# Loads in written order, a later start of the side loads, up factors kept on chip and a ring of three gate tiles in a hybrid HGRN2 and short-convolution block

## The chip, the core and the metric

One core of a Trainium2 chip runs the whole kernel in one launch. TensorE (PE in the profile) multiplies, VectorE (DVE) and ScalarE (ACT) work on tiles in SBUF, GpSimd (POOL) and SyncE (SP) mostly issue transfers. The metric is the device time of one launch in microseconds; the time before is the median of three runs.

## What is computed

The input x is 1024 positions by 2048 channels, all float32. Cut to what matters:

```
mod = silu(c) @ w_ada + b_ada ;  shift, scale, gate = split(mod, 3)
h = rms_norm(x, g_pre) * (1 + scale) + shift
q, f, i, z_a, bb, cc, vb, z_b = split(h @ w_in, 8)            # 8 x 1024 columns
y_a = rms_norm(hgrn2_chunkwise(q, log f, 1 - f, i), g_head_a) * silu(z_a)
y_b = bb * causal_depthwise_conv(cc * vb) * silu(z_b)
m_a, m_b = split(sigmoid(h @ w_merge + b_merge), 2)           # 2 x 2048 columns
out = (m_a * (y_a @ w_up_a) + m_b * (y_b @ w_up_b)) @ w_o
return x + gate * rms_norm(out, g_post)
```

## The kernel before

Every large product is done in float32 as three matmuls of reduced-precision parts: each operand is split into a high part (a cast on ScalarE) and a low part (a subtraction on VectorE), and high x high, high x low and low x high are added in PSUM (`mm3`, `split_w`, `split_h`). The blocks are multiplied by a seven-product scheme (the products are called p1, p6, p2, p7, p5, p4, p3), so sums and differences of blocks, the factors, are formed on VectorE first.

The stages, in order:

- Opening. 16 pieces of x are loaded, normalised and transposed into xT. `ada_pair(q)`, for q = 0 to 3, loads 16 pieces of w_ada (512 KB each, tile `ada_raw`), multiplies them with silu(c) on TensorE (into `prow`) and VectorE (into `row_v`), and turns the two rows into columns of scale and shift (`pa`, `a_c`, `sh_c`). `factors_a` then scales xT and forms the factors of four products for two of eight groups at a time.
- First sweep. 48 units (`unit_a`), one per pair of 128 columns of w_in and w_merge. Each loads four weight tiles (`w_raw`, five buffers), and does products p1, p6, p2 and p7, 96 matmuls of 128x512. Sums go to DRAM (`s_scr`, `u_scr`) for the second sweep. Beside the units run `factors_b` (the factors of p5, p4, p3, stored to `hb_scr`), `gate_step` (w_ada's third part, 32 loads called `ga_raw`) and `sums_o` (sums of w_o, 32 loads called `wo`).
- Second sweep. The same 48 units with p5, p4 and p3, 72 matmuls each, and the recurrent heads and the convolution. From unit 33 on `y_factors` loads y of a branch, forms its seven factors for four groups (tile `yp`) and stores them to `yf_scr`.
- Up b and up a (`up`): the products with w_up_b, then w_up_a. Each first loads its 28 factors (7 products x 4 groups, 512 KB each) from `yf_scr`, then runs eight steps `du` of seven products, 84 matmuls. In a step the products are combined in `o2` and `ut` and multiplied by two gate tiles `g`, loaded on POOL's queue from `g_scr`. Up b stores the results to `pb_scr`; up a adds them back (`merge`, tile `pb`) and stores to `m_scr`.
- Last stage: the product with w_o, the last norm, the store.

Two things set the order. Transfers wait in order in the queue that issues them: most loads in SP's, stores and gate loads in POOL's. Instructions of each engine are put in order by a scheduler that runs the program through a timeline of its own; only what is marked with `keep_in_program_order` stays as written, and `issue_after` holds what is inside it behind a given instruction. At most eight loads are under way from SP's queue: the ninth is issued when the first has landed. Most large tiles (x, xT, w_ada pieces, factors, y, gates) share one pool of 38 buffers of 128x1024 (`big`), so a load also waits until such a buffer is released.

## Time and profile before

| | |
|---|---|
| median of three runs | 2771.5 us (2767.51 to 2771.66) |
| the profiled run | 2769.2 us |
| its span | 2767.5 us |
| mean granted TensorE clock | 0.984 |
| TensorE busy | 97% of the span |
| VectorE busy | 62% |
| ScalarE busy | 33% |
| read from and written to HBM | 431.04 MB, 198.18 MB |

The profile was taken in the run of 2769.2 us. TensorE's busy share is near the whole span, so the mean shares say little; the table of windows, which counts each engine's instructions in a stretch, shows where TensorE is behind its own pace. A window's row begins with the stretch and its length in us, then gives busy us and the number of instructions in brackets for PE, PEld, DVE, ACT and POOL, then the granted clock (1.00 is 2.4 GHz, 0.50 is 1.2 GHz), the busy share of the transfer engines and GB/s. A busy share a little above 1 means that they are full.

### The profile page before, as it was taken

What the parts mean: (1) busy time and instruction counts of PE and PEld (TensorE: products, weight loads), DVE (VectorE), ACT (ScalarE), POOL (GpSimd) and SP (SyncE); (2) the same over time, 40 slices, a digit from 0 to 9 for tenths busy, and PEclk for the clock granted to TensorE, in tenths of its full rate; (3) what the DMA queues carried; (4) which work ended last, traced back from release to release, by engine and by line L of the source; (5) the groups of instructions that cost most, each with busy time, mean ns of one, the idle gap of its engine ahead of it and who ended that gap; (6) DMA issues with size and microseconds to landing.
All of it is one profiled execution on the core that took longest, in us unless ns stands there. A gap on an engine that the chain in (4) does not pass through costs nothing.

```text
span 2767.5 us, 31307 instructions
## 1 busy us (share of the span) xinstructions
PE 2673.0 (97%) x11851; PEld 2152.7 (78%) x11851; DVE 1716.7 (62%) x2096; ACT 906.3 (33%) x1176; POOL 280.0 (10%) x495
## 2 busy tenths in 40 slices
PE   4889999999999999999999999999998999999997
PEld 3267878888888888888888888888885787888786
DVE  6777886754554444546666666656563666765667
ACT  4433222222222222233344444435442222232333
POOL 2012111110000000010000000002111101100000
PEclk9899999999999999999999999999998999999999
DMA  9769999985556655584444444359999569773353
GB/s 361 286 201 313 345 349 364 346 292 179 179 192 179 182 175 177 174 316 137 133 130 133 138 146 138 110 178 374 360 363 407 187 213 335 235 282 99 99 178 142
DMA packets 420071, 631.30 MB, mean 228 GB/s; under 512 B 19564, under 2 KB 281808, under 8 KB 419792
## 3 DMA queue, kind: packets, MB, share of 16 engines
q1 hardware_dynamic: 358528, 394.31, 44.7%
q0 software_dynamic: 60208, 230.78, 21.7%
q10 hardware_dynamic: 1184, 4.20, 0.4%
q8 instruction: 93, 1.52, 0.2%
q14 instruction: 58, 0.48, 0.0%
HBM read 431.04 MB, written 198.18 MB: 227 GB/s over the span
## 4 chain that ended last, share of the span: by engine, by line
PE 81%; issue 8%; DMA 7%; DVE 2%; POOL 1%; ACT 1%; DVEq 0%; POOLq 0%; ACTq 0%; SPq 0%
PE po L866 10%; PE pz L119 7%; PE pz L122 7%; PE pz L123 7%; PE px L119 6%; PE px L123 6%; PE px L122 6%; PE py L123 6%; PE py L119 6%; PE py L122 6%; PE pw L119 4%; PE pw L122 4%; PE pw L123 4%; DMA yp<-yf_scr 3%; DMA ga_raw<-in_w_ada_dram 2%
## 5 line engine op out<-in xcount | busy, mean ns | idle before, releaser
L130 ACT CAST w_hi<-w_raw 128x1024 fp32r<-128x1024 f32 (+1 forms) x296 | 290.9, 983 | 1001.6 <-PE px L122 402.5
L131 DVE TENSOR_TENSOR w_lo<-w_raw,w_hi 128x1024 fp32r<-128x1024 f32 (+1 forms) x296 | 335.7, 1134 | 273.1 <-ACT w_hi L130 263.4
L123 PE MATMUL py<-fp,w_lo 128*128 128x512 f32 x768 | 301.2, 392 | 6.9 <-DVE w_lo L131 6.9
L123 PE MATMUL px<-fp,w_lo 128*128 128x512 f32 x768 | 300.9, 392 | 5.2 <-DVE w_lo L131 5.2
L119 PE MATMUL px<-fp,w_hi 128*128 128x512 f32 x768 | 301.2, 392 | 0.0
L122 PE MATMUL py<-fp,w_hi 128*128 128x512 f32 x768 | 299.5, 390 | 1.3 <-DVE fp L136 1.3
L119 PE MATMUL py<-fp,w_hi 128*128 128x512 f32 x768 | 299.8, 390 | 0.9 <-ACT w_hi L130 0.9
L122 PE MATMUL px<-fp,w_hi 128*128 128x512 f32 x768 | 300.0, 391 | 0.0
L866 PE MATMUL po<-w_hi,lt 128*128 128x512 f32 x896 | 244.2, 390 | 0.6 <-DVE og L900 0.6
L866 PEld LDWEIGHTS po<-w_hi,lt 128*128 128x128 f32 x896 | 168.1, 188 | 37.2 <-DVE og L900 2.2
L130 ACT CAST w_hi<-s 128x512 fp32r<-128x512 f32 (+1 forms) x112 | 90.1, 805 | 285.9 <-PE py L122 245.5
L123 PEld LDWEIGHTS py<-fp,w_lo 128*128 128x128 f32 x768 | 144.5, 188 | 41.5 <-DVE w_lo L131 11.2
L123 PEld LDWEIGHTS px<-fp,w_lo 128*128 128x128 f32 x768 | 144.8, 188 | 36.9 <-DVE w_lo L131 6.5
L122 PEld LDWEIGHTS py<-fp,w_hi 128*128 128x128 f32 x768 | 144.5, 188 | 32.1 <-DVE fp L136 1.7
L122 PEld LDWEIGHTS px<-fp,w_hi 128*128 128x128 f32 x768 | 145.1, 189 | 30.8 <-issue 0.5
L119 PEld LDWEIGHTS px<-fp,w_hi 128*128 128x128 f32 x768 | 144.9, 189 | 30.8 <-issue 0.7
L119 PEld LDWEIGHTS py<-fp,w_hi 128*128 128x128 f32 x768 | 144.5, 188 | 30.8 <-ACT w_hi L130 1.3
L119 PE MATMUL pz<-fp,hi 128*128 128x512 f32 x384 | 152.5, 397 | 3.0 <-DVE d L701 3.0
L122 PE MATMUL pw<-fp,w_hi 128*128 128x512 f32 x384 | 150.8, 393 | 0.0
L119 PE MATMUL pz<-fp,w_hi 128*128 128x512 f32 x384 | 150.5, 392 | 0.0
L123 PE MATMUL pz<-fp,lo 128*128 128x512 f32 x384 | 150.4, 392 | 0.0
L119 PE MATMUL pw<-fp,w_hi 128*128 128x512 f32 x384 | 150.4, 392 | 0.0
(286 smaller groups left out, 4959.4 us busy)
## 6 DMA issues: line engine op xcount, KB each, us to landing
w_raw<-in_w_in_dram SPq DMA_DIRECT2D x160, 512.0 KB, 5.2
s_scr<-s POOLq DMA_DIRECT2D x96, 512.0 KB, 6.0
s_raw<-s_scr SPq DMA_DIRECT2D x96, 512.0 KB, 4.3
w_raw<-in_w_merge_dram SPq DMA_DIRECT2D x80, 512.0 KB, 5.7
u_scr<-o POOLq DMA_DIRECT2D x48, 768.0 KB, 7.5
ada_raw<-in_w_ada_dram SPq DMA_DIRECT2D x64, 512.0 KB, 10.8
yf_scr<-yp POOLq DMA_DIRECT2D x56, 512.0 KB, 9.0
yp<-yf_scr SPq DMA_DIRECT2D x56, 512.0 KB, 12.8
```

The source lines that it names most:

```text
L119: mm = nc.tensor.matmul(o, ah, bh, start=first, stop=False, skip_group_check=True)
L122: nc.tensor.matmul(o, ah, bl, start=False, stop=False, skip_group_check=True)
L123: nc.tensor.matmul(o, al, bh, start=False, stop=last, skip_group_check=True)
L130: nc.scalar.copy(out=hi, in_=raw)
L131: nc.vector.tensor_sub(out=lo, in0=raw, in1=hi.bitcast(F32))
L866: nc.tensor.matmul(o, a, b[:, c], start=st, stop=sp, skip_group_check=True)
```

## The change

- Opening. A helper `load` pins a load in written order on SP. The loads of x, of w_ada, of the weights of units 0 and 1, of the gates' w_ada part and of w_o go through it. w_ada pieces of q = 0, 1, 2 use the shared pool only; of q = 3 every fourth has a tile of its own. The row tiles move into a weight buffer.
- Unit 0 is split: three of its weight splits and the loads of its weights stand ahead of `ada_pair(3)`, and its products p1, p6 and p2 run on factors 0 to 5 first, then on 6 and 7, once the last factors are issued.
- First sweep. `factors_b` runs with units 2 to 16, held behind the unit's last sum; `gate_step` with units 10 to 25; `sums_o` with units 26 to 40 (before: units 0 to 15, 16 to 31, 32 to 46, as far as the scheduler left them there).
- Sides of the second sweep. Branch a's factors for all groups come first, branch b's second; p1 of branch b stays on chip (`first_y`, four tiles), so up b loads 24 factors.
- Up. Gate tiles come from a ring of three buffers of their own instead of the shared pool. `merge`'s loads of pb are pinned.

```diff
+    def load(o, i):
+        tc.keep_in_program_order(nc.sync.dma_start(out=o, in_=i))
...
-        if n_ada[0] % 3:
+        if q < 3 or n_ada[0] % 4:
             raw = bigt(F32, "ada_raw").rearrange("p (k e) -> p k e", k=2)
         else:
-            raw = ph.tile([P, 2, HS], F32, tag="ada", name="ada_raw", bufs=4)
-        nc.sync.dma_start(out=raw, in_=w_ada_v[:, k:k + 2, t, q * HS:(q + 1) * HS])
+            raw = ph.tile([P, 2, HS], F32, tag="ada", name="ada_raw", bufs=2)
+        load(raw, w_ada_v[:, k:k + 2, t, q * HS:(q + 1) * HS])
...
+    def unit_a(u, raws):
...
+        if u == 0:
+            v.tensor_sub(out=a21, in0=a11, in1=a21)
+            w2 = split_w(a12, out_t=(ph.tile([P, 8, P], F32R, name="hi3a", bufs=1), wp.tile([P, 8, P], F32R, tag="raw", name="lo3a", bufs=5)))
+            yield
+            p2 = ps("mm", "p2")
+            for gs in (range(6), (6, 7)):
+                for p, w, f in ((px, w1, "p1"), (py, w6, "p6"), (p2, w2, "p2")):
+                    product(p, w, fa[f], pin=True, gs=gs)
...
     for q in range(1, 4):
+        if q == 3:
+            first = unit_a(0, load_a(0))
+            next(first)
         ada_pair(q)
         factors_a((2 * q - 2, 2 * q - 1))
-    factors_a((6, 7), vec=(7,))
+    with tc.issue_after(factors_a((6, 7), vec=(7,)).ins):
+        next(first, None)
...
     for u in range(NU):
-        unit_a(u)
-        if u < 16:
-            if u % 2 == 0:
-                factors_b(u // 2)
-        elif u < 32:
-            gate_step(2 * u - 32)
-            gate_step(2 * u - 31)
-        elif u % 2 == 0:
-            sums_o((u - 32) // 2)
+        if u:
+            for _ in unit_a(u, load_a(u)):
+                pass
+        if u in range(2, 18, 2):
+            with tc.issue_after(last_sum[0]):
+                factors_b(u // 2 - 1)
+        if 10 <= u < 26:
+            gate_step(2 * u - 20)
+            gate_step(2 * u - 19)
+        elif u in range(26, 42, 2):
+            sums_o((u - 26) // 2)
...
                 split_h(t, factor(s, ys[0], ys[1], lambda: small("t2")), nc.scalar.copy)
+                if br and s == "p1":
+                    first_y.append(t)
+                    continue
...
-    side = [f for g in range(4) for br in (1, 0) for f in y_factors(br, g)]
+    first_y = []
+    side = [f for br in (0, 1) for g in range(4) for f in y_factors(br, g)]
...
-        fy = {s: [pair(f"y{s}_{g}") for g in range(4)] for s in STAGES}
+        fy = {s: [pair(f"y{s}_{g}") for g in range(4)] for s in STAGES if not (y0 and s == "p1")}
+        if y0:
+            fy["p1"] = first_y
...
-                t = bigt(F32, "g")
+                t = ph.tile([P, S], F32, tag="g", name="g", bufs=3)
...
-            nc.sync.dma_start(out=t, in_=pb_scr[2 * du + j])
+            tc.keep_in_program_order(nc.sync.dma_start(out=t, in_=pb_scr[2 * du + j]))
```

SP's queue in the opening, behind the last piece of x. A piece of w_ada is named by a running number: before, 714 and 716 are the first two in written order, 722, 732, 746 and 756 later ones of q = 0, and 1175 to 1329 weights of units 0 and 1.

```order
L180 DMA x_7_1_429<-in_x_dram 128x1024
L224 DMA ada_raw_722<-in_w_ada_dram 128x2x512
L224 DMA ada_raw_732<-in_w_ada_dram 128x2x512
L224 DMA ada_raw_746<-in_w_ada_dram 128x2x512
L224 DMA ada_raw_756<-in_w_ada_dram 128x2x512
L325 DMA w_raw_1175<-in_w_in_dram 128x8x128
L325 DMA w_raw_1177<-in_w_in_dram 128x8x128
L325 DMA w_raw_1179<-in_w_in_dram 128x8x128
L325 DMA w_raw_1181<-in_w_in_dram 128x8x128
L325 DMA w_raw_1329<-in_w_in_dram 128x8x128
L224 DMA ada_raw_714<-in_w_ada_dram 128x2x512
```

The same place in the changed kernel, where 712 is the first piece.

```order
L119 DMA x_7_1_428<-in_x_dram 128x1024
L119 DMA ada_raw_712<-in_w_ada_dram 128x2x512
L119 DMA ada_raw_714<-in_w_ada_dram 128x2x512
L119 DMA ada_raw_720<-in_w_ada_dram 128x2x512
L119 DMA ada_raw_722<-in_w_ada_dram 128x2x512
```

The pieces now follow in written order, and the weights of unit 0 have moved back, to where the pieces of q = 2 end (961 and 963) and those of q = 3 begin (1047):

```order
L119 DMA ada_raw_961<-in_w_ada_dram 128x2x512
L119 DMA ada_raw_963<-in_w_ada_dram 128x2x512
L119 DMA w_raw_1017<-in_w_in_dram 128x8x128
L119 DMA w_raw_1019<-in_w_in_dram 128x8x128
L119 DMA w_raw_1021<-in_w_in_dram 128x8x128
L119 DMA w_raw_1023<-in_w_in_dram 128x8x128
L119 DMA ada_raw_1047<-in_w_ada_dram 128x2x512
```

The first gate loads stand in SP's queue before between the weights of unit 6 (26 weight tiles have been issued):

```order
L365 DMA ga_raw_3640<-in_w_ada_dram 128x2x512
L325 DMA w_raw_2052<-in_w_in_dram 128x8x128
L365 DMA ga_raw_3645<-in_w_ada_dram 128x2x512
L365 DMA ga_raw_3786<-in_w_ada_dram 128x2x512
L365 DMA ga_raw_3790<-in_w_ada_dram 128x2x512
L365 DMA ga_raw_3931<-in_w_ada_dram 128x2x512
L325 DMA w_raw_2054<-in_w_in_dram 128x8x128
```

and now between those of unit 13 (53 have been issued):

```order
L311 DMA w_raw_3077<-in_w_in_dram 128x8x128
L119 DMA ga_raw_2761<-in_w_ada_dram 128x2x512
L311 DMA w_raw_3079<-in_w_in_dram 128x8x128
L119 DMA ga_raw_2766<-in_w_ada_dram 128x2x512
L119 DMA ga_raw_2907<-in_w_ada_dram 128x2x512
L311 DMA w_raw_3081<-in_w_in_dram 128x8x128
```

They have moved by seven units, and the 32nd of them stands behind unit 25's weights where it stood behind unit 11's.

POOL's queue at the start of up b. Gates g_scr16 and g_scr17 are those of step 0, 18 and 19 of step 1, 20 and 21 of step 2; pb_scr0 and pb_scr1 are the results of step 0, and so on. Before:

```order
L740 DMA g_14662<-g_scr18_223 128x1024
L740 DMA g_14664<-g_scr19_224 128x1024
L740 DMA g_14801<-g_scr20_225 128x1024
L664 DMA g_scr30_235<-d1_14309 128x1024
L740 DMA g_14803<-g_scr21_226 128x1024
L740 DMA g_14940<-g_scr22_227 128x1024
L740 DMA g_14942<-g_scr23_228 128x1024
L740 DMA g_15079<-g_scr24_229 128x1024
L781 DMA pb_scr1_238<-g_14525 128x1024
L781 DMA pb_scr0_237<-g_14523 128x1024
```

and after:

```order
L773 DMA g_14644<-g_scr18_223 128x1024
L693 DMA g_scr30_235<-d1_14299 128x1024
L814 DMA pb_scr1_238<-g_14507 128x1024
L814 DMA pb_scr0_237<-g_14505 128x1024
L814 DMA pb_scr2_239<-g_14644 128x1024
L773 DMA g_14646<-g_scr19_224 128x1024
L773 DMA g_14783<-g_scr20_225 128x1024
L773 DMA g_14785<-g_scr21_226 128x1024
L814 DMA pb_scr3_240<-g_14646 128x1024
L773 DMA g_14922<-g_scr22_227 128x1024
L814 DMA pb_scr5_242<-g_14785 128x1024
L773 DMA g_14924<-g_scr23_228 128x1024
```

Nine gates were asked for ahead of the first result's store; now three are, and the second gate of step 1 (g_scr19) stands behind the store of that step's first result (pb_scr2).

## Rows read from the trace of the kernel before

**Rows 1.** The page, busy us of TensorE, its share of the span, instructions.

```profile
PE 2673.0 (97%) x11851; PEld 2152.7 (78%) x11851; DVE 1716.7 (62%) x2096; ACT 906.3 (33%) x1176; POOL 280.0 (10%) x495
```

**Rows 2.** Windows: pace of TensorE in five stretches.

```profile
142.00:174.00 32.00, 25.86 (x97) 20.00 (x97) 26.80 (x36) 12.56 (x18) 2.73 (x5) 0.89 0.52 159
174.00:450.00 276.00, 268.07 (x1161) 218.40 (x1160) 219.71 (x254) 74.99 (x95) 43.46 (x81) 0.99 0.97 329
500.00:550.00 50.00, 50.00 (x222) 41.42 (x221) 32.31 (x30) 12.17 (x15) 6.94 (x13) 1.00 1.04 349
2050.00:2200.00 150.00, 136.40 (x544) 105.76 (x543) 72.66 (x107) 40.05 (x57) 20.92 (x39) 0.91 0.88 331
2250.00:2350.00 100.00, 95.46 (x406) 75.67 (x405) 64.59 (x95) 22.61 (x39) 9.15 (x17) 0.98 0.84 310
```

**Rows 3.** Waits of TensorE: us in total, times, longest us.

```profile
PE prow L235 <- DMA ada_raw<-in_w_ada_dram: 19.5, 4, 15.6
...
PE py L123 <- DVE w_lo L131: 7.5, 6, 2.7
PE pz L119 <- DMA yp<-yf_scr: 6.5, 6, 2.5
```

**Rows 4.** Timeline of SP's queue, opening: start us, us, what, how many.

```profile
16.14 4.21 SPq L224 DMA_DIRECT2D ada_raw<-in_w_ada_dram  x4
24.48 10.04 SPq L325 DMA_DIRECT2D w_raw<-in_w_in_dram  x5
34.56 91.41 SPq L224 DMA_DIRECT2D ada_raw<-in_w_ada_dram  x60
```

**Rows 5.** Windows: the opening.

```profile
0.00:142.00 142.00, 96.73 (x323) 39.28 (x323) 98.18 (x177) 61.08 (x97) 16.56 (x21) 0.87 0.89 315
...
56.00:72.00 16.00, 0.50 (x2) 0.00 (x0) 1.62 (x3) 0.00 (x0) 0.00 (x0) 0.65 1.05 387
...
92.00:132.00 40.00, 36.48 (x100) 9.84 (x99) 32.44 (x56) 20.33 (x31) 0.00 (x0) 0.91 0.99 361
```

**Rows 6.** Timeline of TensorE, end of the opening.

```profile
138.62 0.87 PE L235 MATMUL prow<-ada_raw,c_act 128*1 128x512 f32 x1
...
142.04 0.48 PE L119 MATMUL px<-fp,w_hi 128*128 128x512 f32 x1
```

**Rows 7.** Transfers issued from 0 to 150 us: KB each, median us to landing.

```profile
ada_raw<-in_w_ada_dram SPq DMA_DIRECT2D x64, 512.0 KB, 10.8
```

**Rows 8.** Groups by line, 100 to 145 us: busy us, mean ns of one.

```profile
L136 DVE TENSOR_TENSOR fp<-xT,fp 128x512 fp32r<-128x512 f32 x16 | 10.2, 682 | 0.0
```

**Rows 9.** VectorE's waits from 174 to 450 us, and SP's queue there.

```profile
DVE s L338 <- DMA w_raw<-in_w_in_dram: 19.1, 8, 5.3
...
265.57 7.98 SPq L365 DMA_DIRECT2D ga_raw<-in_w_ada_dram  x4
```

**Rows 10.** Timelines of SP and POOL at up b's start, and a window.

```profile
2099.17 5.44 SPq L728 DMA_DIRECT2D yp<-yf_scr  x5
...
2110.62 12.23 SPq L728 DMA_DIRECT2D yp<-yf_scr  x6
...
2107.20 0.55 POOL L740 DMA_DIRECT2D g<-g_scr  x1 [2.98 <-PE pz L123]
...
2117.04 0.54 POOL L740 DMA_DIRECT2D g<-g_scr  x1 [1.76 <-DMA g<-g_scr]
...
2108.00:2140.00 32.00, 23.77 (x71) 14.85 (x70) 10.75 (x17) 4.50 (x7) 4.83 (x9) 0.72 1.03 409
```

**Rows 11.** Transfers issued from 2020 to 2180 us.

```profile
yf_scr<-yp POOLq DMA_DIRECT2D x15, 512.0 KB, 9.0
```

**Rows 12.** The gate tile, 2100 to 2320 us (ns min/median/max), its landing; the copy.

```profile
L771 DVE TENSOR_TENSOR g<-g,o x9: 1217/1220/1226, 2146.7 to 2316.4; 128x1024 f32<-128x1024 f32 x9
L776 DVE TENSOR_TENSOR g<-g,ut x9: 679/684/687, 2155.7 to 2318.2; 128x512 f32<-128x512 f32 x9
...
DMA to landing us min/median/max: 2.9/6.4/20.1
...
L758 ACT COPY o<-px 128x512 f32<-128x512 f32 x6 | 3.5, 587 | 12.5 <-PE px L123 9.0 <-DVE g L771 3.5
```

98 lines of the change are left out of this document (52 added, 46 removed).

## The prediction, made before the changed kernel ran

> **What bounds the kernel now.** I read the page's busy shares first: TensorE is busy 97% of the span [rows 1], so nothing is won except where it stands still or runs slowly. Where that is comes from the table of windows, by counting matmuls. A window in the middle of the first sweep holds 222 in 50 us at a full granted clock [rows 2], 0.225 us each. Against that pace: 142 to 174 us holds 97 where 142 fit, 45 x 0.225 = 10.1 us lost; 174 to 450 us holds 1161 where 1225 fit, 14.5 us; 2050 to 2200 us (end of sweep two, start of up b) 544 of 666, 27.5 us; 2250 to 2350 us (from up b into up a) 406 of 444, 8.6 us. With the opening, whose first product starts at 142.04 us [rows 6], that is where time can be had; the rest of the span runs at pace. The waits of TensorE [rows 3] name what it stood for: w_ada pieces (19.5 us, 15.6 of it at once), a split's low part on VectorE, and y factors coming back from DRAM.
>
> In the opening the queue of SP shows why: four w_ada loads, then ten microseconds in which five weight tiles of units 0 and 1 are issued one by one, then sixty w_ada loads up to 125.97 us [rows 4]. From 56 to 72 us TensorE starts 2 matmuls while the transfer engines are full at 387 GB/s [rows 5]: what it needs is somewhere behind. Then from 73 to 142 us they have stretches with little to do: all in all 315 GB/s over the first 142 us [rows 5].
>
> **Opening, about -19 us.** All loads now stand in the order of use, and the queue is 16 x + 48 w_ada + 4 weight tiles + 16 w_ada = 84 loads of 524,288 bytes. At 387 GB/s one takes 1.355 us, so 113.8 in all; with the first issue at 0.8 and some 3 us for the first to land, the last lands at 117.6. Before, the last was issued at 125.97 and landed a median 10.8 us later [rows 7], 136.8; the last prow matmul began at 138.62 and the first product at 142.04, 5.2 behind the landing [rows 6]. The same tail puts it at 122.8: -19.2. Loads 23 to 44 wait for the slots of x tiles that the transposes release, by my reading up to 5 us behind the pace; the seven loads in flight cover 7 x 1.355 = 9.5 us, so I charge nothing; without that cover it is those 5 us. Bounds: the slowest rate of a full stretch, 361 GB/s at 92 to 132 us [rows 5], makes 84 x 1.452 = 122.0 and leaves -11; a shorter tail gives -22. The DMA page of the Trainium skill (DMA: Bandwidth & Descriptors, section "Bandwidth") says that between HBM and SBUF some 358 GB/s binds. The row of 387 GB/s speaks against it for one core alone; by 358 GB/s the sum would have -10 here in place of -19.
>
> **Unit 0, -7.5 us.** It now starts with three products on factors 0 to 5, 54 matmuls or 12.2 us, where it had two, 36 or 8.1 us, and their splits stand ahead of the last ada_pair. In that time factors 6 and 7 must come: 6 activations and 8 splits, each a cast on ScalarE and a subtraction on VectorE; 8 x 0.68 [rows 8] is 5.4 us there. So most of the 10.1 us goes; I leave 2.5 for the first matmuls at 1.2 GHz (granted clock 0.89 in that window). Bounds -3 to -10.
>
> **Units 1 to 12, -10 us of 14.5.** Loads of ga_raw stand in SP's queue from 265 us on, between the weights of units 6 to 11 [rows 9], and with their 512 KB each the engines are full; VectorE waits 19.1 us for w_raw there [rows 9]. Now they come with units 10 to 26, two per unit, and one unit's own traffic (4 weights, s, u: 3.9 MB in 21.7 us, 181 GB/s) plus two gate loads is 229 GB/s; with the w_o sums, later, 277, well under 387. Those sums get longer time, not more work. What hides the moved loads is the slack of later units; if it is gone, waits like those of before come back there. But TensorE's stops in this stretch end with VectorE's w_lo [rows 3], some of them at units 2 and 3, before any ga_raw load. I put those down to factors_b on VectorE, which is now held behind the unit's last sum, and count on half of them. Bounds -5 to -13.
>
> **Up b, -16 us of 27.5.** Its 28 factor loads ran 1.28 us apart ((5.44 - 0.32) / 4) while alone, and 2.4 us apart ((12.23 - 0.32) / 5) from 2110 us, when POOL had put nine gate loads beside them from 2107 us on [rows 10]. The engines are full, share 1.03 at 409 GB/s from 2108 to 2140 us [rows 10], and TensorE got 71 matmuls there, half of it at 1.2 GHz (clock 0.72). Now p1 of four groups stays on chip: 4 loads and 4 stores less; and the gates have a ring of three, so six of nine gate loads leave this stretch. Ten transfers of 524,288 bytes at 409 GB/s are 12.8 us that the last factor comes earlier, and with the waits the slow matmuls go: 16. Against it: the queue of branch a's first ten factor loads now follows at once, but behind, in the same queue; and branch b's factors are made last, so its stores end just ahead of their loads (15 such stores of both branches from 2020 us on, 9.0 us to landing [rows 11]). The first of these loads is p6, needed 2.7 us later than p1 was. Bounds -5 to -24.
>
> **Up a, -5 us of 8.6**: ten rather than seven of its factor loads come ahead, and four or more gate loads no longer share the engines. Bounds 0 to -8.6.
>
> **The ring of three, +12 us.** In up b, gates of step 0 and the first of step 1 fill it. The second gate of step 1 stands on POOL's queue behind the store of step 1's first result, which is written after the last product of step 1. Then: 0.69 + 0.68 for the two sums on VectorE, twice 0.54 for the issues, 6.4 to landing (2.9 to 20.1), 1.22 for the product of gate and o2, and 0.59 for the next copy into o2, which has one buffer [rows 12]; 10.7 us after the end of step 1. Step 2's third product adds to the PSUM that this copy must have read; it is due after two products, 24 x 0.225 = 5.4 us. TensorE stops some 5 us. Queued behind the waiting product on VectorE is all of step 2's combining; behind the load on POOL both gates of step 2. In up a the same stands at step 0, with a further sum of pb (1.22): 6.5. With some half-speed matmuls after, 12 together; bounds +4 (landing in 2.9) to +25. From the third step on the load stands a whole step ahead of its use: needed 72 x 0.225 = 16.2 us into the step, there after some 9.
>
> Moving pb's loads and one tile less for rows cost nothing that TensorE waits for: pb is used 16 us into a step. The last stage and the tail are as before.
>
> **Sum.** -19 - 7.5 - 10 - 16 - 5 + 12 = -45.5, on the profiled run's 2769.2 us: 2723.7. The median of the runs is 2.3 above that run, so 2726.
>
> **Rivals.**
> (1) The opening is not bound by the queue's order but by the rate or by VectorE, which is busy 98 us of the first 142 [rows 5] and must do that and two more splits in 123. For it: 80% busy with in-order waits; against: it idled while TensorE waited. Then -11 in place of -19: 2734. The page's 358 GB/s, above, would give 2735.
> (2) Up b stays bound by transfers: stores that come last and branch a's loads take back what the kept factors and gates gave. For it: the engines are full from 2050 us on, before any gate load; against: nine gate loads halved the pace. -5 in place of -16: 2737.
> (3) The ring costs only its lower end and the other terms come to their better ends: 2708.
> (4) The change does not reach what it says: slots, not order, hold the loads of the opening and the gates still crowd the first sweep. -5 and 0 in place of -19 and -10: 2750.
> (5) Slower: the ring holds every step, not the second alone. Each second gate then waits for a store of the step's end, 6 us in each of 16 steps, 96 in place of 12: 2810. It decides from (57.5 / 16) = 3.6 us a step. For it: one queue carries stores and loads in order; against: from step 3 the margin is 7 us.
>
> **How the numbers follow.** Forecast 0.50 (by itself 2714 to 2738), rival (1) 0.12, (2) 0.15, (3) 0.13, (4) 0.04, (5) 0.06. The range reaches from most of (3) over the rest to (4): 2705 to 2750. About 0.2%, 5.5 us, is what a measurement can tell from no change. The worse end of (4), and sums of several worse ends, fall within it: same 0.03; (5) is slower, 0.06; faster 0.91.
>
> **What would show it.** After: the first product near 123 us and no long wait of prow; the end of the first sweep some 36 us earlier; ga_raw loads spread over units 10 to 26, and windows near 222 matmuls per 50 us from unit 1 on; up b's window losing some 11 us where it lost 27.5; and a wait of TensorE of 3 to 7 us in step 2 of up b and step 1 of up a, ended by the copy into o2. It is wrong if transfers idle in the opening while prow waits, if up b's factor loads still come 2.4 us apart, or if a wait for o2 shows in every step.

## The result, and the profile after

The changed kernel takes 2806.65 us (median of four runs, 2802.59 to 2807.85), the kernel before 2769.51 beside it: a ratio of 1.0141, 95% interval 1.0126 to 1.0157. Forecast was 2726. The profiled run took 2807.85 us.

The table follows both traces by the start of the first matmul of each place; "since" is what was won or lost since the line above.

| place | before, us | after, us | difference | since |
|---|---|---|---|---|
| first product | 142.04 | 133.57 | -8.5 | -8.5 |
| unit 1 | 174.23 | 158.40 | -15.8 | -7.4 |
| unit 10 | 382.33 | 359.35 | -23.0 | -7.1 |
| unit 26 | 733.17 | 745.53 | +12.4 | **+35.3** |
| unit 42 | 1082.54 | 1119.64 | +37.1 | **+24.7** |
| second sweep | 1213.65 | 1250.71 | +37.1 | 0 |
| up b, step 2 | 2168.98 | 2194.41 | +25.4 | -11.6 |
| up b, step 3 | 2188.02 | 2220.97 | +33.0 | +7.5 |
| up a | 2283.22 | 2316.16 | +32.9 | 0 |
| up a, step 1 | 2308.72 | 2335.28 | +26.6 | -6.4 |
| up a, step 2 | 2329.72 | 2361.92 | +32.2 | +5.6 |
| last stage | 2443.96 | 2476.16 | +32.2 | 0 |
| its 200th product matmul | 2490.55 | 2529.10 | +38.6 | +6.4 |
| its last matmul | 2752.45 | 2791.04 | +38.6 | 0 |

Up to unit 10 the change wins 23 us. Then 32 units of the first sweep lose 60, and that is the result. The 11.6 us of up b are won almost all before its first matmul, which starts 895.1 us behind the start of the second sweep before and 884.7 after. The page's busy line, against [rows 1], shows none of it: busy shares are the same to a hundredth.

```profile
PE 2682.8 (96%) x11851; PEld 2152.3 (77%) x11851; DVE 1717.3 (61%) x2097; ACT 904.6 (32%) x1175; POOL 278.0 (10%) x491
```

The windows of after answer to [rows 2], with 700 to 1100 us, the stretch of the w_o loads, put in, and up b's window moved by the 37 us that the second sweep starts later (columns as there: stretch, busy us and number of instructions of PE, PEld, DVE, ACT, POOL, granted clock, DMA share, GB/s).

```profile
142.00:174.00 32.00, 30.43 (x132) 24.21 (x131) 17.86 (x19) 7.22 (x9) 2.66 (x5) 1.00 0.60 178
174.00:450.00 276.00, 269.75 (x1174) 220.28 (x1173) 161.95 (x174) 73.60 (x92) 29.24 (x55) 0.99 0.67 217
500.00:550.00 50.00, 47.28 (x201) 38.32 (x200) 31.36 (x36) 12.98 (x16) 5.88 (x11) 0.97 0.73 243
700.00:1100.00 400.00, 380.06 (x1630) 305.36 (x1629) 223.43 (x208) 87.91 (x102) 48.95 (x92) 0.99 0.81 264
2087.00:2237.00 150.00, 136.65 (x562) 106.73 (x561) 74.24 (x108) 38.63 (x55) 16.15 (x31) 0.97 0.86 322
```

The window from 142 us has 132 matmuls where it had 97 (unit 0 starts 8.5 us earlier, and 7.4 us are won in it), up b's has 562 where it had 544, a stop of 7.5 us in step 2 included. But 500 to 550 us, at full pace before (222), has 201; and from 700 to 1100 us 1630 stand where 1776 fit, at a DMA share of 0.81: the transfers are not full.

TensorE's waits (us in total, times, longest) answer to [rows 3]. The long wait for w_ada is gone; the wait of px for a split's low part (the second half of splitting a weight, on VectorE) has become the largest.

```profile
PE px L126 <- DVE w_lo L134: 28.5, 16, 3.8
PE px L209 <- POOL x L203: 16.4, 5, 6.8
PE pa L248 <- DVE row_v L243: 12.5, 3, 4.4
PE py L126 <- DVE w_lo L134: 9.8, 21, 1.5
PE px L122 <- ACT o L791: 7.9, 2, 4.2
PE po L899 <- ACT lt L138: 5.7, 1, 5.7
```

What VectorE itself waits for between 380 and 1110 us points at the moved loads. Before, then after:

```profile
DVE s L338 <- DMA w_raw<-in_w_merge_dram: 63.1, 13, 5.3
DVE s L338 <- DMA w_raw<-in_w_in_dram: 47.0, 13, 5.3
...
DVE gacc L374 <- DMA ga_raw<-in_w_ada_dram: 1.2, 1, 1.2
```

```profile
DVE s L331 <- DMA w_raw<-in_w_in_dram: 70.7, 18, 6.7
DVE s L331 <- DMA w_raw<-in_w_merge_dram: 57.0, 11, 7.0
...
DVE gacc L397 <- DMA ga_raw<-in_w_ada_dram: 38.2, 14, 5.3
DVE wo L416 <- DMA wo<-in_w_o_dram: 31.1, 8, 5.7
```

VectorE waited for weights before, too (110.1 us, now 127.7), but for gate pieces only 1.2 us, and for w_o not at all.

### The profile page after: what moved, and what is told of

The parts are those of the page before. It is cut to its first block, busy times and chain, and to the rows that moved or that the text cites. A ratio compares the mean times of both kernels' runs of the same rounds, so it can differ in the third digit from the quotient of the medians.

```text
span 2806.1 us, 31269 instructions
## 1 busy us (share of the span) xinstructions
PE 2682.8 (96%) x11851; PEld 2152.3 (77%) x11851; DVE 1717.3 (61%) x2097; ACT 904.6 (32%) x1175; POOL 278.0 (10%) x491
## 4 chain that ended last, share of the span: by engine, by line
PE 68%; DMA 15%; DVE 8%; issue 3%; ACT 1%; SPq 1%; DVEq 0%; POOL 0%; ACTq 0%
PE po L899 10%; PE pz L122 7%; PE pz L126 7%; PE pz L125 7%; DMA w_raw<-in_w_in_dram 4%; PE px L122 4%; PE px L126 4%; PE px L125 4%; PE pw L122 3%; PE pw L125 3%; PE pw L126 3%; PE py L126 3%; DMA wo<-in_w_o_dram 3%; PE py L122 3%; PE py L125 3%; DVE w_lo L134 3%
## 5 line engine op out<-in xcount | busy, mean ns | idle before, releaser
L126 PE MATMUL py<-fp,w_lo 128*128 128x512 f32 x768 | 303.6, 395 | 10.1 <-DVE w_lo L134 9.8
L126 PEld LDWEIGHTS py<-fp,w_lo 128*128 128x128 f32 x768 | 144.5, 188 | 51.8 <-DVE w_lo L134 21.9
L331 DVE TENSOR_TENSOR s<-w_raw 128x1024 f32<-128x1024 f32 x48 | 58.8, 1226 | 196.1 <-DMA w_raw<-in_w_in_dram 112.9
```

Source lines behind the costliest of these rows:

```text
L126: nc.tensor.matmul(o, al, bh, start=False, stop=last, skip_group_check=True)
L331: v.tensor_add(out=s1, in0=a21, in1=a22)
```

## Experiments on the first sweep

Two theories. **(A)** VectorE's arithmetic on a gate or w_o piece stands in its order right behind the load; the piece comes late, VectorE waits, and the weights' splits behind it wait too. **(D)** The pinned loads, in SP's queue and in the transfers, hold up the weight loads behind them. The table gives what units 10 to 25 (gates) and 26 to 41 (w_o) take in each run's trace, and where the second sweep starts. A unit at full pace takes 21.8 us. One trace stands for each run, and traces of kernels whose first sweep is written alike differ: in after and the four runs of the next sections that leave its first sweep alone, units 10 to 25 take 379.5 to 386.2 us and 26 to 41 take 374.1 to 379.2; in e1_free and the four that share its first sweep, 363.4 to 369.7 and 350.9 to 352.2. Differences within such a spread say nothing.

| run | units 10-25 | 26-41 | second sweep at | median, us | ratio (interval) |
|---|---|---|---|---|---|
| before | 350.8 | 349.4 | 1213.7 | 2769.5 | |
| after | 386.2 | 374.1 | 1250.7 | 2806.7 | 1.0141 (1.0126-1.0157) |
| e0_place | 351.4 | 350.9 | 1209.4 | 2768.5 | 0.9993 (.9984-1.0002) |
| e1_free | 363.4 | 352.2 | 1205.9 | 2767.4 | 0.9988 (.9977-.9999) |
| e2_ahead | 386.3 | 379.9 | 1256.1 | 2812.3 | 1.0149 (1.0134-1.0164) |
| e2b_lead | 383.0 | 377.5 | 1252.3 | 2812.0 | 1.0152 (1.0135-1.0169) |
| e11_loads | 363.3 | 379.9 | 1233.1 | 2790.2 | 1.0068 (1.0053-1.0083) |
| e12_sums | 370.5 | 349.7 | 1210.1 | 2765.0 | 0.9978 (.9969-.9987) |
| e18_apart | 383.4 | 393.6 | 1269.0 | 2828.3 | 1.0207 (1.0186-1.0228) |
| e19_both | 442.1 | 376.4 | 1312.1 | 2868.9 | 1.0360 (1.0346-1.0375) |
| e24_apart_loads | 361.8 | 360.0 | 1212.1 | 2770.7 | 0.9997 (.9987-1.0006) |
| e25_early_loads | 365.8 | 352.5 | 1209.8 | 2767.4 | 0.9993 (.9983-1.0002) |

### Is it the pins, or the new places?

e0_place gives the first sweep back its old places and takes the pins off the gate and w_o loads; e1_free takes only the pins off.

```
e1_free: -        load(raw, w_ada_v[... 2 ...])          # gate_step
         +        nc.sync.dma_start(out=raw, in_=w_ada_v[... 2 ...])
         -            load(t, w_o_v[...])                 # sums_o
         +            nc.sync.dma_start(out=t, in_=w_o_v[...])
e0_place: as e1_free, and
         -        if 10 <= u < 26: gate_step(2 * u - 20) ...   # and factors_b, sums_o
         +        elif u < 32: gate_step(2 * u - 32) ...       # as before
```

> The changed kernel with its first sweep as before: gate and w_o loads not pinned, factors_b, gate_step and sums_o written at the units of before. All else as changed (2806.7 us; before 2769.5). Theory A: the 60 us lost between units 10 and 42 come from VectorE, which works in order and waits for ga_raw and wo pieces that were issued only some microseconds earlier, with the split's low part behind it; with the loads hoisted again this goes, and the waits of units 1 to 12 come back (7 us): about 2754. Rival B: the loss comes from the rest of the change (unit 0's early start, weights pinned, tiles moved into the weight buffers), and stays: 2795 or more.

> The changed kernel with the gate and w_o loads no longer pinned, at the units of the change. In the queue of SP the first half of the gate loads stays where it was, since the shared pool has no free buffer for them before factors_b is done; the later ones and all w_o loads move ahead by one to five units. Theory A (just-in-time loads that VectorE waits for): the 24.7 us of units 26 to 42 shrink to under 5 and the 35.3 of units 10 to 26 to some 20: about 2770. Theory C (the position of the arithmetic on VectorE, not the loads, holds the splits): within 5 us of 2806.

Measured 2768.5 and 2767.4. Freed, the same calls at the same place in the program give back 44.7 of the 60 us lost in units 10 to 41: 22.8 with the gates, most of it in units 20 to 25, and 21.9 with w_o. (By the median times it is 39.3.) The other 15.4, of which 12.6 lie in units 10 to 21, belong to the new places: with the old ones (e0_place) units 10 to 41 lose 2, but unit 10 starts at 375.8 and not 358.6. The two places are worth nearly the same in the end.

Where the scheduler puts a free load shows in SP's queue, first and last w_o load of the kernel before, of e1_free and of after (start us, us, what, how many):

```profile
381.44 8.35 SPq L391 DMA_DIRECT2D wo<-in_w_o_dram  x4
...
556.78 0.75 SPq L391 DMA_DIRECT2D wo<-in_w_o_dram  x1
```

```profile
602.48 3.33 SPq L414 DMA_DIRECT2D wo<-in_w_o_dram  x1
...
779.16 0.55 SPq L414 DMA_DIRECT2D wo<-in_w_o_dram  x1
```

```profile
724.31 3.56 SPq L119 DMA_DIRECT2D wo<-in_w_o_dram  x4
...
1049.14 3.93 SPq L119 DMA_DIRECT2D wo<-in_w_o_dram  x4
```

`sums_o` was written with units 32 to 46 before, but its loads had been issued in units 9 to 17. Unpinned in the changed kernel they are issued in units 20 to 28. Pinned, they go out where they are written, less than a unit ahead, in units 25 to 39, and in rows of four. Their arithmetic and their stores move with them.

### Loads earlier than their arithmetic

If (A) is all, loads a unit ahead should do. e2_ahead writes them one unit earlier; e2b_lead pins the weights too, puts gate and w_o loads in front of the unit's work and holds their arithmetic behind the unit's last sum.

```
e2_ahead: +        if 9 <= u < 25: gate_load(2 * u - 18); gate_load(2 * u - 17)
          +        elif u in range(25, 41, 2): sums_load((u - 25) // 2)
e2b_lead: +            raws = load_a(u)          # pinned, then gate_load / sums_load
          +        with tc.issue_after(last_sum[0]): gate_step(...) / sums_o(...)
```

> The changed kernel with each pinned gate and w_o load written one unit ahead of its arithmetic; loads stay pinned, none is taken away. Theory A: what a load needs to land (7 to 13 us) fits into one unit of 21.8 us, so most of the 60 us of units 10 to 42 goes; where buffers of the shared pool are short, up to unit 16, some stays: 2760 to 2775. Theory D (pinned loads hold up the weights behind them in SP's queue): the same number of pinned loads stands among the weights, no gain: 2800 or more.

> The changed kernel with gate and w_o loads still pinned, and the weights pinned too, but each gate or w_o load written behind its unit's weights and ahead of the unit's products, and its arithmetic on VectorE held behind the unit's last sum. So a load now has about a unit (21.8 us) between issue and use, where the changed kernel gives it 8.7 us for ga_raw and 10.5 for wo (median). The earlier attempt to write the loads one unit ahead left those intervals at 9.8 and 10.2, since the order of the queue did not follow. Theory A (VectorE waits for pieces issued too late): the loss of units 10 to 42 falls from 60 us to under 12: 2755 to 2765. Theory D (pinned loads in SP's queue hold up the weights): more is pinned, so 2800 or more.

e2_ahead says nothing: the gap from load to use stayed as it was. In e2b_lead the gap grew from a median of 8.7 us to 34 for gates and from 10.5 to 46 for w_o, VectorE no longer waits for either, and nothing was won. Its SP queue shows why, in units 26 to 41 and after (740 to 1110 us):

```profile
SPq L119 <- DVE w_lo L134: 89.0, 33, 6.2
SPq L119 <- DMA t_scr<-wo: 72.8, 14, 11.3
SPq L119 <- DMA w_raw<-in_w_merge_dram: 66.0, 11, 9.4
```

SP stands 72.8 us behind w_o loads that wait for a buffer (released when a sum's store to t_scr has landed), with weights in the queue behind them. In units 10 to 25 it waits 93.6 us in the same way for gate tiles. One wait was exchanged for another; a lead alone wins nothing here, and the run doesn't tell (A) from (D).

### Loads without arithmetic, arithmetic without loads

```
e11_loads: +            if k: continue                 # one multiplication in eight pieces
           -        v.tensor_sub(out=b22, in0=b22, in1=b12) ...   # the four sums of w_o
e12_sums:  -        load(raw, w_ada_v[...])            # one piece kept, read by all
           -            load(t, w_o_v[...])
```

> The changed kernel with the pinned loads of gates and w_o where they are, but nearly all of their arithmetic left out: one multiplication for each of the gate's four column blocks instead of 32 multiply-adds, and the w_o tiles stored as they were loaded (so gates and output are not the reference's). Before the run the first sweep ends at 1250.7 us in the changed kernel and at 1205.9 us with these loads unpinned. If the loss comes from VectorE (it waits for the late pieces with the weights' splits behind, 78 us of such waits, or carries the arithmetic at a bad place): sweep two starts at 1200 to 1215, total about 2760. If it comes from the loads themselves, which stand in SP's queue in front of weights: sweep two starts at 1235 or later, total 2790 or more.

> The other half: the arithmetic of gates and w_o sums stays at its place, but its loads are left out (all of it reads one gate piece, loaded once and kept, so gates and output are not the reference's). If VectorE's waits for pieces or the loads in SP's queue are the cause: sweep two starts at 1200 to 1215, total about 2760. If the place of the arithmetic on VectorE is the cause, whatever it waits for: sweep two starts at 1235 or later, total 2790 or more.

The two halves of the loss differ. With the gates, leaving out the arithmetic gives back all that the pins cost (386.2 to 363.3), leaving out the loads 15.7 or, given the spread, all: pinned loads alone cost nothing there, nor does arithmetic without them (in units 11 to 20 there), which is (A). With w_o, leaving out the arithmetic gives back nothing (379.9): loads at that place, with the stores that follow them, are enough for the loss, which is (D). e12_sums does not add to it (349.7): without loads to wait for, the w_o arithmetic and its stores went to units 18 to 23, so nothing is left in units 26 to 41. In after itself both are at work with w_o: VectorE waits 31.1 us for the pieces, and 9 of 68 weights of units 25 to 41 take over 9 us to land, where it is 25 of 68 in e11_loads. How the 21.9 us divide is not shown. In after, (A) is seen at 540 us (VectorE's timeline; the brackets give the idle time and what ended it): a gate's sum waits 5.28 us for its piece, and the split queued behind it comes that much later.

```profile
545.76 1.54 DVE L397 SCALAR_TENSOR_TENSOR gacc<-ga_raw,c_act,gacc 128x512 f32<-128x512 f32 x2 [5.28 <-DMA ga_raw<-in_w_ada_dram]
547.21 1.22 DVE L134 TENSOR_TENSOR w_lo<-w_raw,w_hi 128x1024 fp32r<-128x1024 f32 x1
```

(D) is seen in e11_loads around 940 us. SP's queue:

```profile
933.75 0.37 SPq L311 DMA_DIRECT2D w_raw<-in_w_merge_dram  x1
934.17 3.88 SPq L119 DMA_DIRECT2D wo<-in_w_o_dram  x4
942.25 22.84 SPq L311 DMA_DIRECT2D w_raw<-in_w_merge_dram  x4
```

Its transfers issued from 934 to 964 us (KB each, median us to landing):

```profile
w_raw<-in_w_merge_dram SPq DMA_DIRECT2D x4, 512.0 KB, 14.5
wo<-in_w_o_dram SPq DMA_DIRECT2D x4, 512.0 KB, 12.1
t_scr<-wo POOLq DMA_DIRECT2D x4, 512.0 KB, 7.2
```

And VectorE, then TensorE, at the end of it, with the window in between:

```profile
963.47 1.22 DVE L331 TENSOR_TENSOR s<-w_raw 128x1024 f32<-128x1024 f32 x1 [8.35 <-DMA w_raw<-in_w_merge_dram]
```

```profile
942.00:951.00 9.00, 9.00 (x40) 7.24 (x39) 3.25 (x4) 2.31 (x3) 1.60 (x3) 1.00 1.05 360
951.00:964.00 13.00, 13.00 (x59) 10.70 (x57) 2.44 (x3) 2.90 (x4) 1.07 (x2) 1.00 0.81 284
964.00:980.00 16.00, 12.05 (x43) 9.48 (x42) 8.38 (x8) 2.28 (x3) 1.07 (x2) 0.79 0.64 170
```

Four w_o pieces go out within 4 us. They come back as four stores, and the next three weights land 13.6 to 17.6 us after their issue, where e12_sums has a median of 5.4. VectorE stands 8.35 us and TensorE then has 43 matmuls in 16 us where 71 fit. Loads and stores both do it, each by itself: among the gate loads of e11_loads, which have no such stores, a weight issued with none, one, two or three side pieces ahead of it in flight landed after a median 4.8, 5.7, 7.9 and 9.7 us (39, 9, 8 and 4 weights), and in units 17 to 24 of e12_sums, which have the stores but no loads, a weight in flight beside four or more of them took a median 8.9. A page of the Trainium skill (DMA: Bandwidth & Descriptors, section "Queues, rings and completion order") says that each transfer engine takes what stands in one queue row's ring in order, and takes turns between rows. The trace agrees in so far as those weights, issued after the four pieces in the same queue, landed after the last of them (957.6 and later against 950.9).

Why do these units not bear it? It is tempting to read it from VectorE, which in the w_merge units stands in every unit until the next weight has landed. But the kernel before, which has no side load in either stretch, shows nearly the same in both: VectorE's waits from 864 to 1082 us (units 32 to 41), then from 602 to 820 us (units 20 to 29):

```profile
DVE s L338 <- DMA w_raw<-in_w_merge_dram: 48.6, 10, 5.3
```

```profile
DVE s L338 <- DMA w_raw<-in_w_in_dram: 35.0, 9, 4.4
```

Such waits hardly tell the two stretches apart. That the places differ is shown by the next runs; why they do is not.

### In a row, or at the place?

e18_apart writes the pinned loads one by one with two weights between; e19_both does so and holds the arithmetic back, with pinned weights; e24 and e25 change one thing each in e11_loads, where no arithmetic disturbs.

```
e18_apart:       +            if between and n % 2: between[n // 2]()     # in load_a: w w G, w w O
e19_both:        as e18_apart, weights pinned, and
                 +        with tc.issue_after(last_sum[0]): gate_step(...) / sums_o(...)
e24_apart_loads: e11_loads with load_a as in e18_apart
e25_early_loads: e11_loads with
                 -        elif u in range(26, 42, 2): sums_o((u - 26) // 2)
                 +        if u in range(14, 30, 2): sums_o((u - 14) // 2)
```

> The changed kernel, gate and w_o loads still pinned, but written one by one with two weight loads between them (w w G w w G ..., w w O w w O ...) in place of two and four in a row behind a unit. Units 26 to 41 cost 374 us in the changed kernel, 380 with the loads alone, 350 with the sums alone and 352 with the loads unpinned. If what costs is that several of these loads stand in a row in front of a weight load: units 26 to 41 take 348 to 358 us, units 10 to 25 some 365 to 375 (386 in the changed kernel), total 2770 to 2785. If it is the pin itself or the amount of loads in these units: units 26 to 41 take 368 or more and the total is 2795 or more.

> The changed kernel, gate and w_o loads pinned, but both one by one between weight loads (w w G w w G, w w O w w O; weights pinned too) and ahead of their arithmetic, which is held behind the unit's last sum. Ahead alone (in rows of two and four) measured 2812.0, apart alone 2828.3. If there are two causes that stand in for each other, VectorE waiting for a late piece, and several pieces in a row in the transfers ahead of a weight: with both taken away units 26 to 41 take 348 to 358 us (374 in the changed kernel), units 10 to 25 at most 370 (386), total 2768 to 2785. If it is neither, but the fixed place itself: units 26 to 41 take 366 or more, total 2795 or more.

> As e11_loads (pinned loads, nearly all arithmetic of gates and w_o sums left out, so the output is not the reference's), but the loads one by one with two weight loads between them. e11_loads: units 26 to 41 take 379.9 us, total 2790.2. If four pieces in a row ahead of a weight are what costs: units 26 to 41 take 348 to 358, total at most 2770. If those units (ten of them the w_merge units, where VectorE's splits are ready just when TensorE wants them) have no room for any further load: 366 or more, total 2780 or more.

> As e11_loads (pinned loads, nearly all arithmetic left out, so the output is not the reference's), but the w_o loads written with units 14 to 28 in place of 26 to 40, in rows of up to four. e11_loads: units 10 to 25 take 363.3 us, 26 to 41 take 379.9, 743.2 together, total 2790.2; with the loads unpinned they were issued from 602 to 785 us (units 20 to 29) and 10 to 41 took 715.6. If the place is what costs (no room in units 32 to 41, room in the earlier ones): units 26 to 41 at most 354, units 10 to 41 at most 722, total at most 2772. If rows of several loads ahead of weights cost wherever they stand: units 10 to 41 take 735 or more, total 2780 or more.

Without arithmetic the answer is plain. One by one, the w_o part falls from 379.9 to 360.0; written twelve units earlier, rows of up to four and all, to 352.5, while units 10 to 25 take 365.8 and not 363.3, which is within the spread. So both: the row makes weights late, and units 32 to 41, most of all, don't bear it. The earlier ones do: in units 14 to 28 of e25_early_loads 30 of 60 weights take over 9 us to land. (The bounds of e24 lay on both sides of 360; the last 10 us, all in units 32 to 41, are the place.)

e18_apart missed, and showed the other theory at work. One by one, few weights are late (in units 25 to 41 two of 68 take over 9 us; in e11_loads 25 of 68), but now the sums wait for their pieces, one of which is issued 8 us before its use:

```profile
1040.92 1.23 DVE L430 TENSOR_TENSOR wo<-wo 128x1024 f32<-128x1024 f32 x1 [6.27 <-DMA wo<-in_w_o_dram]
```

```profile
1047.46 0.79 PE L126 MATMUL py<-fp,w_lo 128*128 128x512 f32 x1 [3.61 <-DVE w_lo L134]
```

e19_both, meant to take both away, missed more widely: the held arithmetic keeps buffers, and SP waited up to 39.7 us for gate tiles with weights behind them. It doesn't settle the question. That a version with pinned loads at these places and neither fault would be as good as e1_free is therefore not shown.

## Experiments on the opening

e7_rowpe moves q = 3's `row_v` from VectorE to TensorE; e17_halfv leaves out every second of VectorE's multiply-adds.

```
e7_rowpe:  +                if q == 3: nc.tensor.matmul(prow2[0:1, :], sc, hr[:, j - k, :], ...)
e17_halfv: +                if j % 2: pass
```

> The changed kernel with row_v of the last quarter of w_ada summed on TensorE, as prow is, and not on VectorE: 16 sums of 0.75 us less on VectorE at the end of the opening, 16 matmuls more on TensorE, which stands idle there. All else as changed (2806.7; first product at 133.6, last w_ada piece landed at about 123.4). Theory: after the last pieces VectorE's chain is what the first product waits for; it comes at 126 to 129, total 2799 to 2803. Rival: the transfers set it, and the first product stays within 1.5 us of 133.6.

> The changed kernel with every second of VectorE's multiply-adds into row_v left out (32 of 64, 0.75 us each, 24 us of VectorE's work in the opening; every w_ada piece is still loaded and read, shift is not the reference's). First product now at 133.57, last piece landed at 123.4. If VectorE's work is what bounds the opening (it also releases the pieces' buffers): first product at 121 to 126. If the rate of the transfers does: last piece lands at 120 or later, and the first product comes at 128 or later, 4.4 us of waiting for row_v being all that goes.

e7_rowpe missed: first product at 136.02, 2815.5 us (1.0159, 1.0145 to 1.0173). TensorE still waited for the sums of q = 1 and 2 (twice, 8.2 us in all), and with the added matmuls it was busy all of 110 to 135 us; the work had only changed its place. The sixteen traces whose opening no edit touches have the first product between 131.1 and 134.7; b3_mix, which has e7_rowpe's edit too, has 135.4. So the edit made it worse, and the -8.5 of the table is -7.3 to -10.9.

e17_halfv has the first product at 126.06, on the edge of what was expected, 5 us ahead of the sixteen. SP's waits from 0 to 130 us for a buffer that such a sum holds, and windows, in after and then in e17_halfv:

```profile
SPq L119 <- DVE row_v L243: 25.4, 12, 8.6
```

```profile
90.00:100.00 10.00, 9.34 (x28) 2.48 (x26) 9.48 (x16) 6.12 (x11) 0.00 (x0) 1.00 1.15 315
...
110.00:120.00 10.00, 9.48 (x20) 1.51 (x18) 9.04 (x14) 4.63 (x7) 0.00 (x0) 0.91 0.88 317
```

```profile
SPq L119 <- DVE row_v L245: 8.7, 7, 2.4
...
SPq L119 <- DVE row_v L243: 4.3, 2, 3.4
```

```profile
90.00:100.00 10.00, 7.18 (x28) 2.87 (x26) 7.72 (x13) 3.33 (x5) 0.32 (x1) 0.87 1.12 302
...
110.00:120.00 10.00, 6.69 (x16) 1.00 (x16) 9.56 (x16) 3.50 (x6) 0.00 (x0) 1.00 1.05 389
```

In after SP waits 25.4 us until VectorE's sums release a buffer, and from 110 to 120 us the transfers fall to a share of 0.88 (0.85 to 1.01 in the sixteen). With half the sums SP waits 13.0 us and the share stays above 1. What is clear of the spread is the tail: the first product follows the last w_ada piece by 3.1 us, in the sixteen by 7.3 to 7.8. That piece lands at 122.97 (after: 125.81; the 123.4 quoted above is the last that prow needs, to within half a us), which is hardly earlier than in the sixteen (123.4 to 127.0). So half of VectorE's sums are shown to cost some 4.5 us behind the last landing; what they cost ahead of it is not.

## Experiments on the up products and the last stage

e5_sides puts the sides back in the old order and drops `first_y`; e3_gbig takes the gates back into the shared pool; e21_ring4 and e13_best are e1_free with a ring of four and with the shared pool; e23_best is e21_ring4 with other addresses.

```
e5_sides:  -    side = [f for br in (0, 1) for g in range(4) for f in y_factors(br, g)]
           +    side = [f for g in range(4) for br in (1, 0) for f in y_factors(br, g)]
e3_gbig:   -                t = ph.tile([P, S], F32, tag="g", name="g", bufs=3)
           +                t = bigt(F32, "g")
e13_best:  e1_free with e3_gbig's line
e21_ring4: e1_free with bufs=4
e23_best:  e21_ring4 with s1 to s4, o2, ut made ahead of g, and gg after the first lt
```

> The changed kernel with the side factors in the order of before and p1 of branch b stored and loaded like the others (28 loads in up b); ring of three and all else as changed. Theory: the changed kernel's up b starts better by some 11 us because of four loads and four stores less and p1 at hand; then this is 2812 to 2820. Rival: the start of up b is better because of the ring alone (three gate loads beside the factors, not nine); then within 3 us of 2806.7.

> The changed kernel with the gate tiles from the shared pool again, the ring of three undone; all else as changed. Theory: the two stops for the copy into o2 (7.5 us in step 2 of up b, 5.6 in step 1 of up a) go, and six gate loads come back beside the factor loads of up b, which costs up to 9 us there: 2794 to 2803. Rival: the ring is not what stops those steps, and the time stays within 2 us of 2806.7 or rises by the 9.

> The changed kernel with the gate and w_o loads unpinned and the gate tiles of the up products back in the shared pool (ring undone). Unpinned alone measured 2767.4; undoing the ring alone gave 7.2 us after the start of sweep two. Sum: about 2760, ratio 0.996 to 0.998. If the gates in the shared pool take back more of up b than that: 2767 or more.

> The changed kernel with gate and w_o loads unpinned and a ring of four gate tiles in place of three. Unpinned with three measured 2767.4 us, with the gates in the shared pool 2757.4. If a step's gates had to wait because three tiles don't hold two steps: both stops of up (7.5 and 5.6 us) go, up b keeps its early start, total 2750 to 2757. If the stop comes from the store and its landing whatever the ring's length: it moves to the next step and stays, total 2765 or more. The last stage's 6.4 us, which stands for the landing of the last store of a ring tile, may stay in either case.

> The changed kernel with gate and w_o loads unpinned, a ring of four gate tiles, and the tiles of the up products put in another order in memory, so that the left factors of the last stage lie over the sums s1 to s4 and o2 and not over gate tiles. With the ring of four alone 2752.9, with a 6.6 us wait at the start of the last stage, 8 us lost there. If that wait comes from the gate tiles' last stores having to land: it goes, total 2743 to 2747. If the last stage is late for another reason (its m tiles, its weights): 2750 or more.

**Sides.** e5_sides: 2810.1 us (1.0141, 1.0127 to 1.0155). Up b's first matmul comes 10.1 us later than in after, but by step 1 only 3.7 are left, 6.0 at step 2 and 5.2 at step 3. From the start of the second sweep to step 2 of up b it is 955.3 us before, 949.8 with the ring alone (this run), 950.6 with the sides alone (e3_gbig) and 943.7 with both. The sides are worth 5 to 6 us of the 11.6, half of what was expected, and the ring the rest.

**The ring.** e3_gbig: 2802.8 us (1.0131, 1.0106 to 1.0156), and both stops are gone. In after the stop is this (POOL's queue, then VectorE, ScalarE and TensorE, around step 2 of up b):

```profile
2199.99 0.53 POOL L814 DMA_DIRECT2D pb_scr<-g  x1 [16.26 <-DVE g L809]
2200.51 1.08 POOL L773 DMA_DIRECT2D g<-g_scr  x2
2203.27 0.54 POOL L773 DMA_DIRECT2D g<-g_scr  x1 [1.69 <-DMA pb_scr<-g]
```

```profile
2208.33 1.22 DVE L804 TENSOR_TENSOR g<-g,o 128x1024 f32<-128x1024 f32 x1
```

```profile
2209.58 0.58 ACT L791 COPY o<-px 128x512 f32<-128x512 f32 x1 [2.62 <-DVE g L804]
```

```profile
2210.22 0.50 PE L122 MATMUL px<-yp,w_hi 128*128 128x512 f32 x1 [3.68 <-ACT o L791]
```

The store of step 1's first result goes out when the step is done, three gate loads follow it in the queue, the last of them once the store has landed; the product of gate and `o2` starts 5.1 us after that load's issue, the copy comes behind it, and TensorE stands 3.68 us (4.2 in up a; against the kernel before, and with half-speed matmuls, 7.5 and 5.6 in all). A fourth tile was enough: e21_ring4 took 2752.9 us (0.9930, 0.9912 to 0.9947), no wait of px on `o` is left, and from step 2 of up b on every step takes 19.0 us but two of up a (19.4 and 20.7). e13_best (shared pool) took 2757.4 (0.9949, 0.9934 to 0.9964): no stops either, but up b's first step takes 45.3 us and not 37.8.

**The last stage.** TensorE waits 5.7 us in after (6.6 in e21_ring4) for a left factor, and ScalarE's waits from 2440 to 2500 us say what that waited for:

```profile
ACT lt L138 <- DMA m_scr<-g: 4.0, 1, 4.0
```

By the order of allocation `lt` lies where a gate tile of the ring lay, and is written only when that tile's store has landed. In e23_best it lies over tiles that no transfer reads. That wait is gone (1.8 and 1.7 us remain, for other things), and the first 200 matmuls take 49.3 us and not 54.5. The other runs agree: the wait for m_scr is there in after, e1_free and e21_ring4, and not in e3_gbig and e13_best, which have no ring, nor in e5_sides, which has the ring but not `first_y`'s tiles. The total of e23_best didn't follow: 2753.1 (0.9937, 0.9923 to 0.9950), since the first sweep of that trace ends 5.9 us later than e21_ring4's. No edit touches that part; the five traces that share it end it between 1205.9 and 1212.2 us, and e23_best's is the latest. Why is open.

**All at once, an early try.** b3_mix freed gate, w_o and pb loads, took the gates from the shared pool two steps ahead in a pinned order of POOL's queue, with e7_rowpe's edit.

```
b3_mix: +                tc.keep_in_program_order(nc.gpsimd.dma_start(out=t, in_=g_scr[n + j]))   # two steps ahead
```

> A mix: the changed kernel with gate, w_o and pb loads not pinned; gate tiles of up from the shared pool, fetched two steps ahead in a pinned order on POOL's queue (results of a step stored, then the two gates of the step after next); row_v of the last quarter on TensorE. If the terms add up: 39 us for the loads (as measured without the pins), 13 for the two stops of the ring, 6 for the last stage, 5 for VectorE's chain in the opening, so 2740 to 2748 against 2769.5 before. If gate loads in up b collide with the factor loads as before, up to 6 more.

2779.4 us (1.0030, 1.0019 to 1.0041), a miss: the first sweep and up b keep their gain, but the first step of up a loses 14 us, all of it in TensorE's waits for y factors. All 28 factor loads of up a are issued from 2271.24 us on, 6 us ahead of its first matmul; e21_ring4 issues the first eleven from 18 us ahead of it. What holds them back here was not tried.

## Why the prediction was wrong

**Units 1 to 12 and the moved loads** is the step that failed. It gave -10 and said that the slack of later units hides the moved loads. Units 1 to 9 did win 7.1. Then units 10 to 41 lost 60.1: 15.4 that the new place costs even with the loads unpinned, 22.8 with the pinned gate loads, whose sums wait for a piece just issued, and 21.9 with the pinned w_o loads, in rows ahead of weights and, in part, with sums that wait for them. The reckoning compared traffic with the transfers' rate (277 against 387 GB/s) and found room, and there was room: a DMA share of 0.81. From 359 to 746 us e1_free even moves 305 GB/s, where after moves 240 and is slower. What lacked room was time: a unit has five weight buffers and four weights, and in e11_loads VectorE stood 8.35 us for a weight that landed some 8 us late. The prediction named its own condition ("if it is gone, waits like those of before come back there"), but no row was read on the later units' slack. And the pins were not weighed at all: [rows 9] shows ga_raw in the queue at 265 us, far from where it was written, and the w_o loads stood at 381 us. The scheduler had placed them well; `load` took that away. What the 15.4 are was not separated: factors_b, which now reaches units 10 to 17 in all versions but e0_place, was not varied alone. Without the 60.1 the other terms, the last stage among them, come to -21.5, not to -45.5: the forecast would have been too good even so. That the total lies near rival (5)'s 2810 is chance.

**The opening** gave -8.5 (-7.3 to -10.9 over the traces), not -19: rival (1), whose -11 was about right. The last piece landed at 125.8 where 117.6 was reckoned, and the tail was 7.8, not 5.2. By e17_halfv the tail is VectorE's: with half its sums it is 3.1. Even then the last piece lands 5.4 us later than reckoned, though the transfers are full from 70 to 120 us: 387 GB/s does not hold over 84 loads, least of all over the four weight tiles in the middle (302 from 90 to 100 us). The 358 GB/s of the Trainium skill (DMA: Bandwidth & Descriptors, section "Bandwidth") gave -10, nearer than the row of 387. The same section gives that figure as a core's part when both cores of a memory domain stream, and one core works here; as a limit it does not hold, since from 30 to 70 us after moved 386 GB/s.

```profile
30.00:70.00 40.00, 34.97 (x137) 13.57 (x138) 27.38 (x51) 15.82 (x24) 2.59 (x2) 0.96 1.05 386
```

**Unit 0**: -7.4 for -7.5. **Up b**: -11.6 for -16, within its bounds. Its factor loads, where they come in a row, are (18.42 - 0.32) / 11 = 1.65 us apart and not 2.4, and the granted clock of its stretch is 0.97 for 0.91; but its first step still takes 38.6 us (39.1 before), so the slow start was not shortened, it began 10.4 us sooner.

```profile
2123.46 18.42 SPq L761 DMA_DIRECT2D yp<-yf_scr  x12
```

**Up a**: -6.4 for -5. **The ring**: +13.1 for +12, by the mechanism described, and in the two steps named; TensorE stood 3.7 and 4.2 us and not 5 and 6.5, the rest was half-speed matmuls. In part that is luck: in up b the copy ended 15.8 us after the end of step 1 and not 10.7, and TensorE had four products to do before it needed it, not two. Rival (5), the slower one, did not happen: steps from the third on are flat.

**The last stage** was put down as unchanged and lost 6.4: the term stood at nothing, and no row was read on which tile the next stage's `lt` would lie over.

With the first sweep as e1_free has it, the other terms stand, and the same change with one more gate tile is 0.7% faster than the kernel before (e21_ring4).

## What to carry to other kernels

Before pinning a load, look in the queue where it stands now, not where it is written: a scheduler may have put it far ahead. Whether other units have room for it can't be read from the transfers' share (0.81 here), nor, as it turned out, from how often VectorE waits there for a weight; moving the loads and measuring the units did show it. And a load wants a lead over its use and no urgent load right behind it; mending one of the two alone gained nothing in the whole kernel (e2b_lead, e18_apart).

## What the hardware showed

- Rows of four 512 KB loads, with the four stores that follow them, delay what is issued behind them in the same queue far longer than the loads' own time: weights landed after 13.6 to 17.6 us instead of 5.4, at an average of 298 GB/s from 934 to 964 us.
- Weight tiles (128x8x128) move more slowly than w_ada pieces of the same size: the windows with the four weight tiles show 315 and 302 GB/s at a DMA share of 1.15 and 1.12, the one with w_ada alone, from 30 to 70 us, 386 at 1.05.
